# A gated convolution and attention block: the input projection as Strassen products of halves, attention as a stage of its own, the convolution's sum in PSUM

## Chip, cores and metric

One core of one Trainium2 chip. The kernel is one program that reads its inputs from HBM and writes one output there. The metric is the device time of one execution in microseconds; lower is better. Engines are named as in the profile: PE multiplies matrices (PEld loads its weights), DVE and POOL work on vectors, ACT applies functions and copies, SP issues most DMAs. SBUF is the working memory, PSUM holds what PE writes.

## What is computed

`x` has 1024 positions of 1024 channels, all float32. One layer, cut to what matters:

```python
h = rms_norm(x, g_pre)
glu_in, gate_a, q, k, v, gate_b, merge = split(h @ w_in)      # 9216 columns
a, b = split(glu_in)
u = depthwise_causal_conv(a * sigmoid(b), conv_w, 31 taps) + conv_b
y_a = (silu(layer_norm(u, ln_g, ln_b)) * silu(gate_a)) @ w_conv_proj
# 8 heads, two softmax maps each, keys of the same or earlier chunks of 64;
# the first 16 of 64 dims of q and k are rotated by the position
p1, p2 = softmax(q1 @ k1.T / 8), softmax(q2 @ k2.T / 8)
o = rms_norm((p1 - lam * p2) @ v, g_subln) * (1 - lambda_init)
y_b = (o * silu(gate_b)) @ w_attn_proj
m_a, m_b = split(merge)
out = (sigmoid(m_a) * y_a + sigmoid(m_b) * y_b) @ w_out
return x + rms_norm(out, g_post)
```

## The kernel before

**Precision.** PE reads float32 in a rounded form (`fp32r`). Each factor is therefore split into an upper part (H) and what is left (L), and each product is three: H with H, H with L, L with H (`product`, lines 235 to 241). A split is a copy on ACT and a subtraction, on POOL for weights (lines 213, 214).

**Projection.** The normalised `x` is transposed and split once: eight tiles `hH` and eight `hL`, each 128 channels by 1024 positions (lines 287 to 291). The 9216 columns of `w_in` come in blocks of 128 (`weight_blocks`). A block takes, for each half of the positions, 8 contraction tiles x 3 products of 128 x 512 (`project`). The values are the exception: they are wanted with the positions on the partitions, so `hH` and `hL` are the stationary side there, and the products are 256 columns wide (`values`). After each block DVE and ACT turn the sum in PSUM into a gate, a gated unit or rotated queries and keys. Queries and keys go to DRAM whole and are split after they are read back, by ACT and POOL (`stacks`, lines 400 to 403).

**Convolution.** `conv` (lines 607 to 617) adds 31 shifted, scaled copies of a tile of 128 channels, one DVE instruction over 1024 positions for each tap. Input, running sum and output lie in SBUF. It is called at a low priority, so that it fills DVE's gaps.

**Heads.** `head` takes two blocks of 128 queries at a time. For each block and map: scores in PSUM, their maximum (line 441), the exponential with its sum (444); then the second map is scaled by ACT (450), the two are joined by DVE (451), transposed by PE (458), split by ACT and DVE (460, 461) and multiplied by the values (470). The squares for the norm are split (478, 480) and summed over channels by PE with a matrix of ones (481, 482); the norm's factor is applied after all heads (649).

**Order.** `PLAN` names groups of projection blocks; one group follows each pair of heads, so that projection and attention run beside each other. Layer norm, the convolution's gate and attention's projection (`attn_out`) come after the last heads, then the convolution's projection and the output projection. The instructions of each engine stand in a fixed order that a planner writes from estimated times and from priorities. All loads and nearly all stores are issued from SP's queue, in order too. Weights are made one block ahead.

Of the kernel before, what the change touches and what calls it, by code (L numbers as in the profile page):

```python
# [11 lines left out]
F32 = mybir.dt.float32  # L12
# [8 lines left out]
P = 128  # L21
# [19 lines left out]
def weight_blocks():  # L41
    """Order of the projection's column blocks: name -> (index, columns, contraction tiles)."""
    blocks = []
    for p in range(4):
        maps = [(2 * p + i // 2, i % 2) for i in range(4)]
        q0 = [OFF_Q + h * P + m * HD for h, m in maps]
        k0 = [OFF_K + h * P + m * HD for h, m in maps]
        rope = [b + half * 8 + j for half in range(2) for j in range(8) for b in q0 + k0]
        rest = [b + d for d in range(ROPE, HD) for b in q0 + k0]
        blocks.append((("qk", p, 0), rope, range(8)))  # L50
        for n in range(3):
            blocks.append((("qk", p, n + 1), rest[n * P:(n + 1) * P], range(8)))
        cols = list(range(OFF_V + p * 256, OFF_V + (p + 1) * 256))
        blocks.append((("v", p, 0), cols, range(0, 4)))
        blocks.append((("v", p, 1), cols, range(4, 8)))
    for name, off in (("a", OFF_A), ("b", OFF_B), ("ga", OFF_GA), ("gb", OFF_GB),
                      ("ma", OFF_MA), ("mb", OFF_MB)):
        for i in range(8):
            blocks.append(((name, i), list(range(off + i * P, off + (i + 1) * P)), range(8)))
    return blocks  # L60


@with_exitstack
def block_kernel(ctx, tc, x, positions, vecs, conv_w, lambdas, g_subln, g_post,
                 w_in, w_cp, w_ap, w_out, out):
    nc = tc.nc
    sb = lambda name, bufs=1: ctx.enter_context(tc.tile_pool(name=name, bufs=bufs))
    const = sb("const")
    hpool = sb("hpool", 16)
    wpool = sb("wpool", 2)  # L70
    half = sb("half", 6)
    tmp_pool = sb("tiny", 4)
    upool = sb("upool", 2)
    cpool = sb("cpool", 1)
    dram = ctx.enter_context(tc.tile_pool(name="dram", bufs=1, space=DRAM))
    ps = ctx.enter_context(tc.tile_pool(name="ps", bufs=2, space=PSUM))
# [4 lines left out]
    PLAN = ("v0 g0 g1|"  # L81
# [5 lines left out]

    def psum_g():
        return ps.tile([P, HALF], F32, name="ps_g", tag="g", bufs=2)

    def psum_s():
        return ps.tile([P, 2, HALF], F32, name="ps_s", tag="s", bufs=2)

    def halftile(name="hf", tag="hf", bufs=4):
        return half.tile([P, HALF], F32, name=name, tag=tag, bufs=bufs)

    def sidetile(name, dt=F32):
        return half.tile([P, 256], dt, name=name, tag="ha", bufs=6)

# [12 lines left out]
    lamv = apool.tile([P, 4, HD], F32, name="lamv", tag="K", bufs=2)  # L112
# [9 lines left out]
    ones_er = const.tile([P, P], F32R, name="ones_er")  # L122
# [4 lines left out]
    pat = half.tile([P, 2, 8, 8], F32, name="pat", tag="hf", bufs=4)  # L127
# [7 lines left out]
    pat2 = half.tile([P, 16, 8], F32, name="pat2", tag="hf", bufs=4)  # L135
# [6 lines left out]
    nc.vector.memset(col[64:128, 2:3], -1.0)  # L142

# [1 line left out]
    lam = const.tile([P, 4], F32, name="lam")  # L145
    ltmp = half.tile([P, 2, HD], F32, name="ltmp", tag="hf", bufs=4)
# [10 lines left out]
    def rsqrt_small(v, r):  # L157
        """r = v ** -0.5 for a few columns: root of the reciprocal, then one Newton step."""
# [11 lines left out]
    wsrc = {}  # L170
    for i, (key, _, _) in enumerate(weight_blocks()):
        wsrc[key] = w_in[i]
    for i in range(8):
        wsrc[("ap", i)] = w_ap[i]
        wsrc[("cp", i)] = w_cp[i]

    def group(name, *idx):
        return [(name, i) for i in idx]

    def pair(p):  # L180
        return [("qk", p, n) for n in range(4)]

    def vpair(p):
        return [("v", p, 0), ("v", p, 1)]

    def glus(*idx):
        return [(n, i) for i in idx for n in ("b", "a")]

    def parse(text):
        keys = []  # L190
        for tok in text.split():
            k, i = tok[0], int(tok[1])
            keys += {"u": glus(i), "q": pair(i), "v": vpair(i), "g": group("gb", i), "m": group("ma", i),
                     "n": group("mb", i), "s": group("ga", i), "p": group("ap", i)}.get(k, [(k, i)])
        return keys

    plan = [parse(x) for x in PLAN.split("|")]
    start = [("qk", 0, n) for n in (1, 2, 3, 0)] + plan[0]
    head_fill = plan[1:]
    order = start + sum(head_fill, [])  # L200
    order = [k for k in order if k[0] not in "tlw"] + group("cp", *range(8))
    loaded = {}
    nextw = [0]
    AHEAD = 2

    def split(src, wH, wL, eng=None, parts=1):
# [3 lines left out]
        n = D // parts  # L210
        for c in range(parts):
            sl = slice(c * n, (c + 1) * n)
            nc.scalar.copy(out=wH[:, sl], in_=raw[:, sl])  # L213
            (eng or nc.gpsimd).tensor_tensor(out=wL[:, sl], in0=raw[:, sl], in1=wH.bitcast(F32)[:, sl],  # L214
                                             op=ALU.subtract)

    def load_weight(parts=1):
        if nextw[0] >= len(order):
            return
        key = order[nextw[0]]  # L220
        nextw[0] += 1
        wL = wpool.tile(blk, F32R, name="wL", tag="wL")
        wH = wpool.tile(blk, F32R, name="wH", tag="wH")
        split(wsrc[key], wH, wL, parts=2 if key[0] == 'v' and key[2] == 1 else parts)
        loaded[key] = (wH, wL)

    def weight(key):
# [3 lines left out]
        while nextw[0] < len(order) and len(loaded) < AHEAD - 1:  # L231
            load_weight()
        return r

    def product(acc, lH, lL, rH, rL, n=8, tiles=None):
        """acc += sum over (some of) the n contraction tiles of l.T @ r, both in two parts."""
        for d in tiles or range(n):
# [572 lines left out]
```

## Time and profile before

| | us |
|---|---|
| Median of 3 runs | 1339.72 |
| Lowest and highest run | 1338.58, 1340.38 |
| Span of the profiled execution, first to last instruction | 1333.2 |

The profile gives for the profiled execution its span alone; 6.5 us lie between that and the median of the runs. A group of the profile names line, engine and operation, the tile written and the tiles read, shapes, then count, busy time and mean duration in ns, and the engine's idle time before it. Matmuls overlap in the pipeline, so the distance of their starts, not their duration, is what one costs. By stages: the first 32 us bring `x` in and normalise it, from there to 985 us projection and heads run together, then the attention output is normalised and the convolution's branch follows, the convolution's projection among it, and the output projection ends the kernel.

### The profile page before, as it was taken

What the parts mean: (1) busy time and instruction counts of PE and PEld (TensorE: products, weight loads), DVE (VectorE), ACT (ScalarE), POOL (GpSimd) and SP (SyncE); (2) the same over time, 40 slices, a digit from 0 to 9 for tenths busy, and PEclk for the clock granted to TensorE, in tenths of its full rate; (3) what the DMA queues carried; (4) which work ended last, traced back from release to release, by engine and by line L of the source; (5) the groups of instructions that cost most, each with busy time, mean ns of one, the idle gap of its engine ahead of it and who ended that gap; (6) DMA issues with size and microseconds to landing.
All of it is one profiled execution on the core that took longest, in us unless ns stands there. A gap on an engine that the chain in (4) does not pass through costs nothing.

```text
span 1333.2 us, 16733 instructions
## 1 busy us (share of the span) xinstructions
PE 1258.1 (94%) x6352; PEld 1060.5 (80%) x6352; DVE 938.6 (70%) x1267; ACT 509.5 (38%) x926; POOL 375.1 (28%) x170
## 2 busy tenths in 40 slices
PE   4999998989998999999899999999999889999998
PEld 3898876868886887987778888888888668887886
DVE  6513699999969979998996695658616881256433
ACT  5424533532254354224435413656534431122211
POOL 2142232243215115212521422241122453233000
PEclk9999999989998999999899999999999999999999
DMA  5342223342123324122324515144349774345222
GB/s 197 122 145 81 88 83 111 107 138 81 58 87 111 115 91 134 64 64 73 118 76 139 154 60 174 64 135 154 127 156 327 235 258 173 115 154 175 91 84 95
DMA packets 61944, 167.16 MB, mean 125 GB/s; under 512 B 7924, under 2 KB 12580, under 8 KB 61864
## 3 DMA queue, kind: packets, MB, share of 16 engines
q1 hardware_dynamic: 61544, 165.82, 38.2%
q8 instruction: 50, 0.82, 0.3%
q10 hardware_dynamic: 288, 0.26, 0.1%
q14 instruction: 30, 0.25, 0.1%
q0 software_dynamic: 32, 0.02, 0.0%
HBM read 123.00 MB, written 43.07 MB: 125 GB/s over the span
## 4 chain that ended last, share of the span: by engine, by line
PE 44%; DVE 38%; DMA 6%; issue 5%; ACT 2%; POOL 1%; SPq 0%; DVEq 0%; ACTq 0%; POOLq 0%
DVE cv L615 23%; PE ps_g L239 10%; PE ps_g L241 10%; PE ps_g L240 10%; DVE nm L441 2%; PE ps_s L724 2%; PE ps_s L725 2%; PE ps_s L726 2%; PE ps_av L470 2%; DVE wtL L461 2%; PE ps_s L435 1%; PE ps_s L436 1%; DVE e L451 1%; DMA qkraw<-qk_dram 1%; PE ps_t L458 1%
## 5 line engine op out<-in xcount | busy, mean ns | idle before, releaser
L214 POOL TENSOR_TENSOR wL<-wraw,wH 128x1024 fp32r<-128x1024 f32 (+1 forms) x93 | 237.9, 2560 | 674.7 <-ACT wH L213 655.5
L239 PE MATMUL ps_g<-hH,wH 128*128 128x512 f32 (+1 forms) x1040 | 408.4, 393 | 13.2 <-DVE qkst L363 4.7
L241 PE MATMUL ps_g<-hH,wL 128*128 128x512 f32 (+1 forms) x1040 | 406.5, 391 | 0.0
L240 PE MATMUL ps_g<-hL,wH 128*128 128x512 f32 (+1 forms) x1040 | 406.3, 391 | 0.0
L615 DVE SCALAR_TENSOR_TENSOR cv<-u,cw,cv 128x1024 f32<-128x1024 f32 x240 | 375.5, 1565 | 2.6
L239 PEld LDWEIGHTS ps_g<-hH,wH 128*128 128x128 f32 x1040 | 196.9, 190 | 54.6 <-DVE qkst L363 5.6
L241 PEld LDWEIGHTS ps_g<-hH,wL 128*128 128x128 f32 x1040 | 197.1, 190 | 38.3
L240 PEld LDWEIGHTS ps_g<-hL,wH 128*128 128x128 f32 x1040 | 197.1, 190 | 37.7 <-issue 0.5
L444 ACT ACTIVATE e<-ps_s,nm 128x256 f32<-128x256 f32 (+7 forms) x128 | 94.9, 742 | 136.2 <-DVE nm L441 108.3
L213 ACT CAST wH<-wraw 128x1024 fp32r<-128x1024 f32 (+1 forms) x93 | 92.7, 1001 | 125.4 <-PE ps_g L240 89.4
L450 ACT ACTIVATE e<-e,rz 128x128 f32<-128x128 f32 (+3 forms) x64 | 49.7, 777 | 122.2 <-DVE rz L449 121.8
L441 DVE TENSOR_REDUCE nm<-ps_s 128x1 f32<-128x640 f32 (+7 forms) x128 | 94.6, 747 | 1.6
L451 DVE SCALAR_TENSOR_TENSOR e<-e,rz 128x128 f32<-128x128 f32 (+3 forms) x64 | 60.4, 943 | 27.2 <-ACT e L450 27.1
L435 PE MATMUL ps_s<-kst,qh 128*128 128x384 f32 (+4 forms) x192 | 66.7, 353 | 4.2 <-ACT e L444 4.2
L461 DVE TENSOR_TENSOR wtL<-ps_t,wtH 128x512 fp32r<-128x512 f32 (+2 forms) x96 | 52.5, 547 | 19.9 <-ACT wtH L460 19.8
L436 PE MATMUL ps_s<-kst,ql 128*128 128x384 f32 (+4 forms) x192 | 64.6, 342 | 0.0
L460 ACT CAST wtH<-ps_t 128x512 fp32r<-128x512 f32 (+2 forms) x96 | 45.6, 475 | 47.4 <-PE ps_t L458 47.1
L492 ACT ACTIVATE th<-ps_g 128x512 f32<-128x512 f32 x80 | 47.3, 593 | 30.4 <-PE ps_g L241 30.2
L239 PE MATMUL ps_g<-ogH,wH 128*128 128x512 f32 x128 | 50.5, 394 | 6.5 <-DVE yb L591 5.9
L458 PE MATMUL ps_t<-ident,e 128*128 128x128 f32 x288 | 49.8, 277 | 6.5 <-DVE wtL L461 4.6
L401 POOL TENSOR_TENSOR kst<-qkraw,kst 64x1024 fp32r<-64x1024 f32 x16 | 44.4, 2774 | 30.7 <-ACT kst L400 20.7
L239 PE MATMUL ps_g<-zH,wH 128*128 128x512 f32 x128 | 49.9, 390 | 1.3 <-DVE tar L707 1.3
(197 smaller groups left out, 2058.4 us busy)
## 6 DMA issues: line engine op xcount, KB each, us to landing
wraw<-w_in SPq DMA_DIRECT2D x72, 512.0 KB, 3.6
qkraw<-qk_dram SPq DMA_DIRECT2D x64, 256.0 KB, 4.2
qk_dram<-qkst SPq DMA_DIRECT2D x32, 256.0 KB, 2.4
xt<-x SPq DMA_DIRECT2D x8, 512.0 KB, 8.2
o_dram<-og SPq DMA_DIRECT2D x32, 128.0 KB, 1.8
u_dram<-th SPq DMA_DIRECT2D x16, 256.0 KB, 2.0
u<-u_dram SPq DMA_DIRECT2D x8, 512.0 KB, 3.8
cv_dram<-cv SPq DMA_DIRECT2D x8, 512.0 KB, 2.6
```

The lines of the kernel that those rows point to most:

```text
L213: nc.scalar.copy(out=wH[:, sl], in_=raw[:, sl])
L214: (eng or nc.gpsimd).tensor_tensor(out=wL[:, sl], in0=raw[:, sl], in1=wH.bitcast(F32)[:, sl], op=ALU.subtract)
L239: nc.tensor.matmul(acc, a, c, start=(d == 0), stop=False)
L240: nc.tensor.matmul(acc, a, e, start=False, stop=False)
L241: nc.tensor.matmul(acc, b, c, start=False, stop=(d == n - 1))
L435: nc.tensor.matmul(sv[:, a, :], qh[:, qs], k[:, ks], start=True, stop=False)
L436: nc.tensor.matmul(sv[:, a, :], ql[:, qs], k[:, ks], start=False, stop=True)
L441: nc.vector.tensor_reduce(out=nm[:, m:m + 1], in_=sv, op=ALU.max, axis=AX.XY, negate=True)
L444: nc.scalar.activation(out=e[:, :n].rearrange("p (a b) -> p a b", a=c), in_=sv, func=AF.Exp, bias=nm[:, m:m + 1], accum_out=Z[:, m:m + 1])
L451: nc.vector.scalar_tensor_tensor(out=es[0][:, :n], in0=es[0][:, :n], scalar=rz[:, 0:1], in1=es[1][:, :n], op0=ALU.mult, op1=ALU.add)
L461: nc.vector.tensor_tensor(out=wtL[g][:, :nk, us], in0=pt[:, :nk, :], in1=wtH[g].bitcast(F32)[:, :nk, us], op=ALU.subtract)
L615: nc.vector.scalar_tensor_tensor(out=a, in0=u[:, k:k + T], scalar=cw[:, i, k:k + 1], in1=a, op0=ALU.mult, op1=ALU.add)
```

## The change

**Seven products of halves.** Two blocks of 128 columns form a pair. Its weights are a matrix of 2 x 2 quarters A (two blocks by two halves of the contraction), the transposed `x` one of 2 x 2 quarters B (halves of the contraction by halves of the positions). The variant used has seven products in place of eight:

- on the side of `x`, made once: T1 = B12 - B11, T2 = B22 - T1, T3 = B22 - B12, T4 = T2 - B21; these and B11, B21, B22 are split
- on the side of the weights, for each pair, by POOL: S1 = A21 + A22, S2 = S1 - A11, S3 = A11 - A21, S4 = A12 - S2; these and A11, A12, A22 are split (ACT and POOL)
- the seven products are combined by ACT and DVE to the four quarters of the result

```diff
+    def factors(tok):
+        raws = []
+        for key in pair_of(tok):
+            raw = proj.tile(blk, F32, name="wraw", tag="raw", bufs=3)
+            nc.sync.dma_start(out=raw, in_=wsrc[key])
...
+        def made(src):
+            f = proj.tile([P, 2, HALF], F32R, name="wf", tag="wf", bufs=8)
+            split(src, f)
...
+        yield made(a11)
+        s1 = total(a21, a22, ALU.add)
+        s2 = total(s1, a11, ALU.subtract)
+        yield made(s2)
+        yield made(total(a11, a21, ALU.subtract, out=a21))
+        yield made(s1)
+        yield made(a12)
+        yield made(a22)
+        yield made(total(a12, s2, ALU.subtract))
...
+    USED = ("B11", "T2", "T3", "T1", "B21", "T4", "B22")
+    def quarters(tok, left, refill):
...
+        step(p1, 0, True)
+        nc.scalar.activation(out=u2, in_=p1, func=AF.Copy, scale=pos)
+        step(p6, 1, True)
+        plus(u2, p6, u2)
+        step(p7, 2, True)
+        plus(u3, p7, u2)
+        step(p5, 3, True)
+        plus(c22, p5, u3)
+        use(i, 1, 1, c22)
+        step(p1, 4, False)
+        step(p4, 5, True)
+        plus(u3, p4, u3, neg)
+        use(i, 1, 0, u3)
+        use(i, 0, 0, p1)
+        step(p5, 6, False)
+        plus(u2, p5, u2)
+        use(i, 0, 1, u2)
+        if k == "u":
+            with tc.high_priority(offset=-20000):
+                conv(i)
```

`made` splits (a copy on ACT, a subtraction on POOL). `step` issues one product, 4 tiles x 3 matmuls of 512 columns, and then has one factor of the next pair made. `plus` is one DVE instruction with one input in PSUM.

The values go through the same products and are then transposed by PE in blocks of 128 (64 transposes in all). Queries, keys and values are split in this stage, and both parts go to DRAM. The products have six banks of PSUM.

**Convolution.** The running sum is a PSUM tile; each tap reads one input from SBUF and one from PSUM. The layer norm's sums and differences move from DVE to POOL, its passes stand between the later pairs:

```diff
-    PLAN = ("v0 g0 g1|"
...
+PLAN = ("u0 g0 u1 g1 q0 u2 q1 q2 u3 q3 q4 u4 q5 q6 u5 q7 s0 u6 s1 s2 u7 s3 v0 v1 v2 v3 "
+        "l0 m0 l1 m1 l2 m2 m3 n0 n1 g2 g3 n2 n3")
...
+        acc = ps.tile(blk, F32, name="cacc", tag="cv", bufs=1)
+        a = wide("cv", "cv", 1)
...
+        for k in range(1, TAPS):
+            nc.vector.scalar_tensor_tensor(out=a if k == TAPS - 1 else acc, in0=u[:, k:k + T],
+                                           scalar=cw[:, i, k:k + 1], in1=acc, op0=ALU.mult, op1=ALU.add)
```

Here u is the gated unit, q queries and keys, s and g the gates, v the values, m and n the merge gates, l the three passes of the layer norm and the convolution's swish.

**Second stage.** After the last pair all pools of that stage are given back, and the eight heads follow. Beside them stands only the convolution's projection (`conv_out`), one or two blocks after each of the heads 0 to 5. The head reads K, Q, V and its gate ready made, joins the two maps without normalising them first, and norms its own output:

```diff
-                nc.scalar.activation(out=es[1][:, :n], in_=es[1][:, :n], func=AF.Copy, scale=rz[:, 1:2])
-                nc.vector.scalar_tensor_tensor(out=es[0][:, :n], in0=es[0][:, :n], scalar=rz[:, 0:1],
-                                               in1=es[1][:, :n], op0=ALU.mult, op1=ALU.add)
+                nc.vector.reciprocal(out=rz[:, 0:1], in_=Z[:, i, 1:2])
+                nc.vector.scalar_tensor_tensor(out=rz[:, 1:2], in0=rz[:, 0:1], scalar=Z[:, i, 0:1], in1=neglam,
+                                               op0=ALU.mult, op1=ALU.mult)
+                nc.vector.scalar_tensor_tensor(out=es[0][:, :n], in0=es[1][:, :n], scalar=rz[:, 1:2],
+                                               in1=es[0][:, :n], op0=ALU.mult, op1=ALU.add)
...
+            nc.gpsimd.tensor_copy(out=sh, in_=sq)
+            nc.gpsimd.tensor_tensor(out=sl_, in0=sq, in1=sh.bitcast(F32), op=ALU.subtract)
+            for u in range(2):
+                us_ = slice(u * P, (u + 1) * P)
+                nc.tensor.matmul(av[:, 1, 2 * u:2 * u + 2], sh[:, us_], ones_er, start=True, stop=False)
+                nc.tensor.matmul(av[:, 1, 2 * u:2 * u + 2], sl_[:, us_], ones_er, start=False, stop=True)
...
+        nc.sync.dma_start(out=ors_dram[h:h + 1, :].rearrange("o (a p) -> p (o a)", p=P), in_=r)
+        rb = apool.tile(blk, F32, name="orb", tag="rb", bufs=1)
+        nc.sync.dma_start(out=rb, in_=ors_dram[h:h + 1, :].broadcast_to([P, T]))
+        nc.gpsimd.tensor_tensor(out=og, in0=og, in1=rb, op=ALU.mult)
```

**Third stage.** Attention's projection (for the first two blocks all heads but the last come first), merged with the convolution's, then the output projection as before.

More of the change, by code (lines that the diff above doesn't have):

```diff
@@ L167, in rsqrt_small @@
         nc.vector.tensor_tensor(out=r, in0=y, in1=q, op=ALU.mult)
[L170 to L200, printed above, removed]
@@ new lines, in block_kernel, with run, refill @@
+    store = {0: ready + list(early)}
+    def run(n):
+        nxt = factors(pairs[n + 1]) if n + 1 < len(pairs) else iter(())
+        store[n + 1] = []
+        def refill():
+            store[n + 1].extend(f for f in [next(nxt, None)] if f is not None)
+        quarters(pairs[n], store.pop(n), refill)
+    done = 0
+    for tok in plan:
+        if tok[0] == "l":
+            ln_part(int(tok[1]))
+        else:
+            if tok == "q0":
+                tables()
+            run(done)
+            done += 1
@@ new lines, in block_kernel, with psum_2, psum_s @@
+    work_cm.__exit__(None, None, None)
+    proj_cm.__exit__(None, None, None)
+    ps_cm.__exit__(None, None, None)
+    wpool = sb("wpool", 2)
+    half = sb("half", 4)
+    bpool = sb("bpool", 16)
+    apool_cm = tc.tile_pool(name="attn", bufs=1)
+    apool = apool_cm.__enter__()
+    ps_cm = tc.tile_pool(name="ps2", bufs=1, space=PSUM)
+    ps = ps_cm.__enter__()
+    def psum_2():
+        return ps.tile(hb, F32, name="ps_g", tag="g", bufs=2)
+    def psum_s():
+        return ps.tile([P, 2, HALF], F32, name="ps_s", tag="s", bufs=2)
@@ L206, in split, with split2 @@
-    def split(src, wH, wL, eng=None, parts=1):
+    def split2(src, wH, wL, eng=None):
         raw = wpool.tile(blk, F32, name="wraw", tag="wr", bufs=2)
         nc.sync.dma_start(out=raw, in_=src)
[L210 to L225, printed above, removed]
+        nc.scalar.copy(out=wH, in_=raw)
+        (eng or nc.gpsimd).tensor_tensor(out=wL, in0=raw, in1=wH.bitcast(F32), op=ALU.subtract)
@@ L230, in weight @@
         r = loaded.pop(key)
-        while nextw[0] < len(order) and len(loaded) < AHEAD - 1:
+        if not loaded:
             load_weight()
         return r
-    def product(acc, lH, lL, rH, rL, n=8, tiles=None):
-        for d in tiles or range(n):
-            a, b, c, e = lH(d), lL(d), rH(d), rL(d)
-            nc.tensor.matmul(acc, a, c, start=(d == 0), stop=False)
-            nc.tensor.matmul(acc, a, e, start=False, stop=False)
-            nc.tensor.matmul(acc, b, c, start=False, stop=(d == n - 1))
@@ new lines, in block_kernel, with psum_3 @@
+    fill = {0: (0,), 1: (1, 2), 2: (3,), 3: (4, 5), 4: (6,), 5: (7,)}
+    for h in range(8):
+        if h == 6:
+            for g in range(6):
+                load_og(g)
+        head(h)
+        for i in fill.get(h, ()):
+            conv_out(i)
+    ps_cm.__exit__(None, None, None)
+    apool_cm.__exit__(None, None, None)
+    cpool = sb("cpool")
+    ypool = sb("ypool", 16)
+    opool = sb("opool", 8)
+    ps = ctx.enter_context(tc.tile_pool(name="ps3", bufs=8, space=PSUM))
+    def psum_3():
+        return ps.tile(hb, F32, name="ps_o", tag="o", bufs=8)
@@ L726, in out_part @@
             nc.tensor.matmul(acc, yL[d][:, ts], woH[d][:, nsl], start=False, stop=(d == 7))
-    halves = [slice(0, HALF), slice(HALF, D)]
-    both = [psum_s() for _ in range(2)]
+    both = [[psum_3() for _ in range(2)] for _ in range(2)]
     for d0, d1 in ((0, 4), (4, 8)):
@@ L739, in block_kernel @@
         if t < 2:
-            accs = [both[t][:, n, :] for n in range(2)]
+            accs = both[t]
         elif t < NT - 1:
-            acc = psum_s()
-            accs = [acc[:, n, :] for n in range(2)]
+            accs = [psum_3() for _ in range(2)]
             for n in range(2):
```

805 lines of the change are left out of this document (412 added, 393 removed), and 5 rows, old and new, of the table PLAN.

## The prediction

> **What bounds the kernel now.** I read the page first: busy shares, the slices, the chain of work that ended last.
>
> ```profile
> span 1333.2 us, 16733 instructions
> PE 1258.1 (94%) x6352; PEld 1060.5 (80%) x6352; DVE 938.6 (70%) x1267; ACT 509.5 (38%) x926; POOL 375.1 (28%) x170
> ...
> PE 44%; DVE 38%; DMA 6%; issue 5%; ACT 2%; POOL 1%; SPq 0%; DVEq 0%; ACTq 0%; POOLq 0%
> ```
>
> TensorE (PE) is busy for 1258.1 us, so 75 us of the span are its idle time. Yet VectorE (DVE) holds 38% of the chain. The windows of 50 us say where that is (columns: PE, weight loads, DVE, ACT, POOL, each with its count, then the clock).
>
> ```profile
> 0.00:50.00 50.00, 31.31 (x199) 28.15 (x200) 32.89 (x76) 26.96 (x47) 9.01 (x23) 1.00 0.42 156
> ...
> 250.00:300.00 50.00, 43.23 (x196) 35.08 (x195) 49.76 (x44) 20.70 (x33) 21.29 (x7) 0.93 0.45 129
> ...
> 400.00:450.00 50.00, 44.53 (x210) 36.31 (x209) 49.67 (x51) 19.49 (x33) 22.15 (x9) 0.93 0.36 108
> ...
> 1100.00:1150.00 50.00, 50.00 (x220) 40.99 (x220) 6.18 (x9) 5.91 (x6) 14.20 (x7) 1.00 0.41 147
> ...
> 1300.00:1350.00 50.00, 26.56 (x139) 22.36 (x137) 11.69 (x34) 5.00 (x17) 0.00 (x0) 0.96 0.19 63
> ```
>
> Three things are to be seen. PE loses 18.7 us in the first 50, and 33.2 - 26.6 = 6.6 us at the end. Between them it is full, except where DVE is full too (49.76 and 49.67 of 50): there PE loses 5 to 7 us a window. And 1100 to 1150 is pure 512-wide matmuls: 50 / 220 = 0.227 us each. So PE's work sets the time, and DVE's convolution costs some PE on top.
>
> **PE's work.** Groups by shape, and two neighbours in the timeline:
>
> ```profile
> L239 PE MATMUL ps_g<-hH,wH 128*128 128x512 f32 x1008 | 399.4, 396 | 13.1 <-DVE qkst L363 4.7 <-DVE sg L517 2.8 <-ACT th L492 2.4
> ...
> L239 PE MATMUL ps_g<-wH,hH 128*128 128x256 f32 x128 | 37.0, 289 | 0.3 <-DVE vL L385 0.3
> ```
> ```profile
> 28.84 0.29 PE L239 MATMUL ps_g<-hH,wH 128*128 128x256 f32 x1
> 28.96 0.28 PE L240 MATMUL ps_g<-hL,wH 128*128 128x256 f32 x1
> ```
>
> The durations (396, 289 ns) overlap; the starts count: 0.227 us for 512 columns, 0.12 for 256. The projection is now 3 x 1008 = 3024 wide ones (687 us) and 768 (the values) + 96 narrow ones (104 us). After: 36 pairs x 7 products x 12 = 3024 wide ones, 687 us. (Today's work is 3024 + 864 / 2 = 3456 wide ones; 7/8 of that is 3024.) The loops leave no doubt about the count; PE is spared the 104 us of the narrow ones. Added: 64 transposes of the values, between 0.12 us (as a narrow one) and 0.23: 8 to 15, I take 8. The other three projections (1152 wide ones) keep 262 us. What is left of the 1258 is 1258 - 791 - 262 = 205: some 190 for the heads.
>
> **What pays for it: POOL.** A pair needs 4 sums and 7 splits, 11 half-row operations on POOL; a block of before needed one full one.
>
> ```profile
> L214 POOL TENSOR_TENSOR wL<-wraw,wH 128x1024 fp32r<-128x1024 f32 x83 | 222.4, 2680 | 632.6 <-ACT wH L213 613.4 <-PE ps_s L436 19.0
> ```
> ```profile
> 72.24 1.29 POOL L364 TENSOR_TENSOR qkst<-qkst,ropet 128x512 f32<-128x512 f32 x1 [4.30 <-DVE qkst L363]
> ...
> 254.10 3.53 POOL L214 TENSOR_TENSOR wL<-wraw,wH 128x1024 fp32r<-128x1024 f32 x1 [12.38 <-ACT wH L213]
> ...
> 1138.97 2.40 POOL L214 TENSOR_TENSOR wL<-wraw,wH 128x1024 fp32r<-128x1024 f32 x1 [8.59 <-ACT wH L213]
> ```
>
> Undisturbed a full one takes 2.40 us, a half one 1.29; at 254 one took 3.53. DVE's line at that time:
>
> ```profile
> 255.51 3.21 DVE L615 SCALAR_TENSOR_TENSOR cv<-u,cw,cv 128x1024 f32<-128x1024 f32 x1
> ```
> ```profile
> L615 DVE SCALAR_TENSOR_TENSOR cv<-u,cw,cv x240: 1196/1284/3496, 163.5 to 799.1; 128x1024 f32<-128x1024 f32 x120
> ```
>
> A tap takes 1.28 us in the median and 3.2 beside POOL: the two hold each other up. Both inputs of that tap lie in SBUF. Beside a DVE operation with one input in PSUM neither is held up:
>
> ```profile
> 866.35 0.69 DVE L527 SCALAR_TENSOR_TENSOR th<-th,ps_g 128x512 f32<-128x512 f32 x1 [0.95 <-ACT th L492]
> ```
> ```profile
> 866.31 2.41 POOL L403 TENSOR_TENSOR ql<-qkraw,qh 128x1024 fp32r<-128x1024 f32 x1
> ```
>
> The taps' running sum moves to PSUM, so they become of that kind, and I take POOL at its undisturbed price. POOL's work in the first stage: 36 x 11 + 32 (queries and keys) = 428 half operations and 31 full ones (sums, mean and variance of the layer norm) = 486 halves. At 1.29 us that is 627 us, 91% of PE's 695. Raw weights have three buffers; a pair's second block waits for the last sum of the pair before it, so POOL idles some 1.5 us a pair (3.6 us of landing less two half operations, by the row below): 54 us more. So POOL comes close to PE, and the layer norm's mean pass puts 36 us of it into four pairs. With one pair of factors made ahead I put PE's loss at 15 us (0 to 60).
>
> By the Trainium skill (GPSIMD Engine Reference, Key points), GpSimd shares its SBUF interfaces with VectorE and contends with instructions there that have two SBUF inputs. The rows at 254 agree; by this rule the taps in PSUM would not contend at all, and the sum would stay as it is.
>
> **What pays for it: DVE.**
>
> ```profile
> L441 DVE TENSOR_REDUCE nm<-ps_s 128x1 f32<-128x1024 f32 x16 | 19.4, 1215 | 0.1
> ...
> L441 DVE TENSOR_REDUCE nm<-ps_s 128x1 f32<-128x512 f32 x16 | 10.9, 680 | 0.2
> ...
> L503 DVE SCALAR_TENSOR_TENSOR th<-th,ps_g 128x512 f32<-128x512 f32 x16 | 10.8, 678 | 1.6 <-PE ps_g L241 1.4
> ```
>
> A tap with its sum in PSUM is not in the trace. From a 512-wide operation on PSUM and SBUF (0.678) and the reductions' step (1.215 - 0.680), it is 1.21 us; twice 0.678 gives 1.36 at most; I take 1.25. Then 248 taps take 310 us. Before the layer norm (26 pairs, 497 us of PE) DVE has also 26 x 5 combinations (88 us), and about 75 us in gates, rotary, values and tables: 473, 95% of PE's time. DVE's queue is in a fixed order, and in the two full windows above such a load cost PE 5 to 7 us in 50. I put PE's loss at 20 us (0 to 45). PSUM's six banks for products hide a late combination of up to about two products; beyond that PE stops.
>
> **Start.**
>
> ```profile
> 21.69 0.80 PE L239 MATMUL ps_g<-hH,wH 128*128 128x256 f32 x2
> ...
> 39.23 1.43 DVE L289 SCALAR_TENSOR_TENSOR hL<-ps_s,vec,hH 128x512 fp32r<-128x512 f32 x2 [1.74 <-ACT hH L288]
> 40.70 1.43 DVE L289 SCALAR_TENSOR_TENSOR hL<-ps_x,vec,hH 128x512 fp32r<-128x512 f32 x2
> ```
> ```profile
> wraw<-w_in SPq DMA_DIRECT2D x72, 512.0 KB, 3.6
> ...
> or<-ors_dram SPq DMA_DIRECT2D x8, 512.0 KB, 5.5
> ```
>
> Now the projection begins at 21.7 us with the first half of the positions. After, only the first product can; the second needs T2, made from both halves, so it waits for the last of x, which before was split by 42.1 us (last row). For the second half DVE then has 18 operations of about 0.7 us (four splits, eight first differences, T2's four sums, two of its splits) where it had 8: 7 us more, of which waits like the 1.74 us in the first row take up some 3. So the second product starts at 46 us (42 to 55); until then PE has only transposes and one product (3 us).
>
> **Heads.** They are a stage of their own, with only the convolution's projection (384 matmuls, 87 us) beside them: PE has 190 + 87 = 277 us. DVE's rows of the heads:
>
> ```profile
> L441 DVE TENSOR_REDUCE nm<-ps_s 128x1 f32<-128x640 f32 (+7 forms) x128 | 94.6, 747 | 1.6
> L451 DVE SCALAR_TENSOR_TENSOR e<-e,rz 128x128 f32<-128x128 f32 (+3 forms) x64 | 60.4, 943 | 27.2 <-ACT e L450 27.1
> ...
> L461 DVE TENSOR_TENSOR wtL<-ps_t,wtH 128x512 fp32r<-128x512 f32 (+2 forms) x96 | 52.5, 547 | 19.9 <-ACT wtH L460 19.8
> ```
> ```profile
> L449 DVE TENSOR_TENSOR rz<-rz,lam 128x1 f32<-128x1 f32 x64 | 28.0, 437 | 1.2
> ...
> L480 DVE TENSOR_TENSOR osql<-osq,osqh 128x256 fp32r<-128x256 f32 x32 | 22.0, 689 | 0.0
> L440 DVE MEMSET ps_s<- 64x64 f32 x128 | 14.0, 112 | 26.9 <-PE ps_s L436 20.3 <-ACT e L444 5.7
> ...
> L475 DVE TENSOR_TENSOR og<-ps_av,sg 128x256 f32<-128x256 f32 x32 | 13.3, 417 | 18.9 <-ACT osq L473 18.9
> ...
> L448 DVE RECIPROCAL rz<-Z 128x2 f32<-128x2 f32 x64 | 10.1, 158 | 14.7 <-ACT e L444 14.4
> ```
>
> They sum to 295 us. L480 goes to POOL (-22); small norm operations come (+16, at L448's price) and the convolution's 16 merges and last splits (+14): 303 us, or about 275 were none held up. So here DVE is the longest. ACT's scaling of the second map (L450) goes, which only shortens the chain. No filler is left for DVE, where today the taps fill every gap; the two score buffers let two query blocks run together. At a head's end the next one's second map waits for free K and Q buffers (1.5 MB). I take 303 us at 92%: 330 (290 to 420).
>
> ```profile
> GB/s 197 122 145 81 88 83 111 107 138 81 58 87 111 115 91 134 64 64 73 118 76 139 154 60 174 64 135 154 127 156 327 235 258 173 115 154 175 91 84 95
> ```
>
> K, Q and V now come already split: 12 loads of 256 KB, V and the gate, 4.5 MB a head, and with z, weights and stores some 65 MB in the stage, 197 GB/s. A slice of today reaches 327 GB/s, so I cost them at nothing; at a head's start, where nothing covers them, they are the bubble that the 92% holds. In the first stage the stores of Q, K and V double (96 of 256 KB); they share SP's queue with weight loads that now wait for a raw buffer, and whatever stands behind such a load waits too, so that the six small work buffers come free late. That costs nothing while POOL keeps its pair of factors ahead; otherwise it is part of the 60 us above. Change of pools before the heads: the first K and Q land in some 4 us after their space is free: 5 us (0 to 20).
>
> **Rest.** Attention's and the output projection: 768 x 0.227 = 175 us, of which I let 12 run in the last head's gaps. The last head's norm chain (a write, the 5.5 us broadcast, POOL, ACT, DVE: some 14 us) lies beside 84 products (19 us). End: 6.6.
>
> **Sum.** 46 + (687 - 3 + 8) + 35 + 5 + 330 + 163 + 7 = 1278 us of span. The median of the runs, 1339.7, stands 6.5 over the span of 1333.2, so **1285**.
>
> **Rivals.**
> 1. Everything hides: stage-one loss 5, no bubble, heads 290, 160 for the rest: 1200 + 6.5 = 1207. For it: PE was at 50.00 of 50 beside a DVE of 30 to 47 us. Against: POOL at 91% and DVE at 95%. 0.20.
> 2. Slower: taps and POOL still hold each other up. Then a half operation costs 2.680 / 2.40 x 1.29 = 1.44 us on average, up to 1.9 (3.53 / 2.40). At 1.56, between, 486 x 1.56 + 54 = 812 us of POOL against 727: 1285 + 85 = 1370. It decides once a half operation passes (695 - 54) / 486 = 1.32 us. 0.13.
> 3. Slower: the heads wait for their own chain (scores, maximum, exponential, sum, transpose), DVE at 72%: 420 us, 1375. For it: no filler. Against: two score buffers. 0.12.
> 4. Slower: PE's clock falls in the heads.
>
> ```profile
> 274.00:278.00 4.00, 1.00 (x5) 0.48 (x3) 3.96 (x2) 1.79 (x3) 3.84 (x3) 0.85 0.53 150
> 278.00:282.00 4.00, 3.12 (x12) 2.93 (x13) 4.00 (x5) 0.00 (x0) 2.70 (x1) 0.50 0.51 135
> 282.00:286.00 4.00, 4.00 (x16) 3.20 (x15) 4.00 (x5) 2.20 (x4) 0.00 (x0) 0.80 0.22 73
> ```
>
> After a gap the granted clock was 0.50, then 0.80: 2.0 + 0.8 = 2.8 us lost. At each of the 32 steps of two query blocks that makes 90 us: 1375, if PE ends last there. Against: DVE does. 0.05. The Trainium skill (TensorE: Matmul & The Clock Gate, the HAM clock gate) says that an idle window of about 3.4 us halves the clock; the rows agree.
>
> The forecast has 0.50, by itself 1245 to 1325. The range over all but the outer tenths is 1210 to 1370. A difference of 0.2% (2.7 us) is about what a measurement can tell. Rivals 2 to 4 hold 0.30; where they strike at under half their price the kernel is still faster (0.05) or equal (0.02). So faster 0.75, same 0.02, slower 0.23.
>
> **What would show it.** Second product near 46 us; PE over 90% to about 770 us, in windows with 0.227 us a matmul; L615's successor near 1.25 us with max and median close; POOL's halves near 1.29; heads near 330 us with DVE over 90%. Wrong would be: halves over 1.4 (rival 2), DVE under 75% in the heads (3), a clock under 0.9 there (4).

## The result: 15% slower, and the profile after

| | before | after |
|---|---|---|
| Median of the runs, us | 1339.15 (1337.09 to 1340.38) | 1544.05 (1542.77 to 1546.25) |
| Span of the profiled execution, us | 1333.2 | 1542.5 |
| Mean granted clock of PE | 0.989 | 0.894 |

The ratio is 1.152, 95% interval 1.149 to 1.155. The forecast was 1285, the range 1210 to 1370. The page of the changed kernel, its busy shares, PE's slices with the clock, and the chain that ended last:

```profile
span 1542.5 us, 16543 instructions
PE 1249.0 (81%) x5616; PEld 1036.0 (67%) x5616; DVE 962.8 (62%) x1490; ACT 549.0 (36%) x1026; POOL 795.8 (52%) x598
...
PE   2799999899999998089989299895665676689998
...
PE 39%; DMA 14%; POOL 14%; DVE 8%; issue 6%; ACT 5%; SPq 1%; POOLq 0%; DVEq 0%; ACTq 0%
```

PE was busy 94% before and is busy 81% now, and DVE has nearly left the chain (38% to 8%), while DMA (6% to 14%) and POOL (1% to 14%) hold more of it. Three places stand out among the slices: the 0 in the middle, the 2 after it, and the stretch of 5 to 7 that follows. The windows of the changed kernel, cut at those places (PE, weight loads, DVE, ACT, POOL, each with its count; clock; DMA share; GB/s):

```profile
0.00:54.00 54.00, 19.94 (x74) 15.51 (x75) 41.55 (x79) 33.97 (x62) 26.83 (x36) 1.00 0.36 132
61.00:611.00 550.00, 527.76 (x2317) 432.82 (x2317) 494.39 (x495) 195.48 (x333) 455.61 (x347) 0.98 0.38 130
611.00:663.00 52.00, 0.71 (x3) 0.41 (x2) 0.69 (x1) 6.73 (x8) 32.33 (x17) 0.53 0.23 76
663.00:849.00 186.00, 178.97 (x760) 145.14 (x759) 70.06 (x75) 69.28 (x112) 138.05 (x91) 0.97 0.45 156
849.00:880.00 31.00, 3.10 (x8) 2.01 (x8) 1.57 (x5) 6.91 (x7) 11.66 (x5) 0.56 1.00 287
880.00:1058.00 178.00, 160.13 (x783) 135.24 (x784) 98.06 (x246) 71.13 (x153) 44.47 (x33) 0.89 0.54 157
1058.00:1345.00 287.00, 173.19 (x856) 151.82 (x857) 168.19 (x441) 122.80 (x273) 53.44 (x55) 0.71 0.41 110
1345.00:1543.00 198.00, 182.46 (x812) 151.40 (x811) 81.29 (x144) 39.50 (x76) 28.90 (x13) 0.96 0.35 117
```

Against the terms of the forecast (heads from their first matmul at 867 to their end near 1350):

| Stretch | forecast, us | measured, us |
|---|---|---|
| start, until the products run steadily | 46 | 61 |
| products of stage 1, losses included | 727 | 788, of which 51 are one stop |
| change of stages | 5 | 18 |
| heads | 330 | 483 |
| rest and end | 170 | 192 |
| span | 1278 | 1542 |

So 153 of the 264 us lie in the heads, 51 in one stop of PE. The heads are of two kinds: on PE all 384 matmuls of the convolution's projection ran between 906 and 1039, beside heads 0 and 1, whose norms leave at 960 and 1047, with PE 90% busy from 880 to 1058; heads 2 to 7 had nothing beside them, and there PE is busy 60% (173.19 of 287 us). Who was waited for stands in the timelines of PE, POOL and SP's queue (start, duration, engine, line, tiles, in brackets the idle time before and its releaser). PE at the stop, at the first matmul of the heads, and at the start of a head in the middle:

```profile
662.59 3.78 PE L421 MATMUL ps_g<-tot,ones_d 128*128 128x512 f32 x4 [51.29 <-POOL tot L439]
...
867.14 0.77 PE L674 MATMUL ps_s<-kst,qh 128*128 128x128 f32 x2 [18.24 <-ACT zH L579]
...
1122.42 0.45 PE L674 MATMUL ps_s<-kst,qh 128*128 128x128 f32 x1 [9.25 <-DMA qh<-qkh]
```

POOL before the stop, and SP's queue before that head:

```profile
647.59 2.34 POOL L434 TENSOR_TENSOR cvr<-cvr,mu 128x1024 f32<-128x1024 f32 x1 [3.38 <-DMA cvr<-cv]
651.09 2.34 POOL L439 TENSOR_TENSOR tot<-tot,cvr 128x1024 f32<-128x1024 f32 x1 [1.17 <-ACT cvr L435]
656.70 2.34 POOL L434 TENSOR_TENSOR cvr<-cvr,mu 128x1024 f32<-128x1024 f32 x1 [3.27 <-DMA cvr<-cv]
```
```profile
1102.46 0.37 SPq L729 DMA_DIRECT2D ors_dram<-orr  x1
1111.41 0.32 SPq L731 DMA_DIRECT2D orb<-ors_dram  x1
1111.82 0.45 SPq L638 DMA_DIRECT2D qh<-qkh  x1
1112.36 0.57 SPq L638 DMA_DIRECT2D kst<-qkh  x1
```

The stop: the matmul that sums the variance stands in PE's queue ahead of the next pair's products, and POOL prepares its input one tile in 9.1 us (647.59 to 656.70: wait for the load, subtract, square on ACT, add; POOL itself works 4.7 us of it). The head: SP writes the norm's factor at 1102.46, the broadcast that reads it back stands in the queue until 1111.41, and the next head's K and Q loads stand behind it.

### The profile page after: what moved, and what is told of

Same layout as the page of the kernel before. It is cut to its first block, busy times and chain, and to the rows that moved or that the text cites. A ratio compares the mean times of both kernels' runs of the same rounds, so it can differ in the third digit from the quotient of the medians.

```text
span 1542.5 us, 16543 instructions
## 1 busy us (share of the span) xinstructions
PE 1249.0 (81%) x5616; PEld 1036.0 (67%) x5616; DVE 962.8 (62%) x1490; ACT 549.0 (36%) x1026; POOL 795.8 (52%) x598
## 4 chain that ended last, share of the span: by engine, by line
PE 39%; DMA 14%; POOL 14%; DVE 8%; issue 6%; ACT 5%; SPq 1%; POOLq 0%; DVEq 0%; ACTq 0%
PE ps_g L471 16%; PE ps_o L604 6%; PE ps_g L604 5%; POOL wf L183 5%; DMA ors_dram<-orr 3%; POOL wsum L202 2%; DMA wraw<-ogd 2%; PE ps_av L710 2%; PE ps_o L822 2%; PE ps_o L823 2%; PE ps_o L821 2%; DVE cacc L408 2%; ACT e L683 2%; POOL qkL L377 2%; DMA ql<-qkl 2%
## 5 line engine op out<-in xcount | busy, mean ns | idle before, releaser
L471 PE MATMUL ps_g<-T,wf 128*128 128x512 f32 x1728 | 406.1, 390 | 4.6 <-DVE T L276 3.9
L471 PEld LDWEIGHTS ps_g<-T,wf 128*128 128x128 f32 x1728 | 324.9, 188 | 73.0 <-DVE T L276 4.3
L471 PE MATMUL ps_g<-B,wf 128*128 128x512 f32 x1296 | 320.5, 400 | 23.8 <-DVE c L483 23.7
L471 PEld LDWEIGHTS ps_g<-B,wf 128*128 128x128 f32 x1296 | 249.4, 193 | 82.0 <-DVE c L483 28.0
L408 DVE SCALAR_TENSOR_TENSOR cacc<-u,cw,cacc 128x1024 f32<-128x1024 f32 x232 | 297.6, 1283 | 2.8
L183 POOL TENSOR_TENSOR wf<-wraw,wf 128x512 fp32r<-128x512 f32 x144 | 198.1, 1379 | 53.8 <-ACT wf L182 53.8
L183 POOL TENSOR_TENSOR wf<-wsum,wf 128x512 fp32r<-128x512 f32 x108 | 149.0, 1380 | 20.3 <-ACT wf L182 20.3
L483 DVE SCALAR_TENSOR_TENSOR u<-ps_g,u 128x512 f32<-128x512 f32 x112 | 76.7, 685 | 80.3 <-PE ps_g L471 75.7
L182 ACT CAST wf<-wraw 128x512 fp32r<-128x512 f32 x144 | 88.5, 618 | 104.6 <-PE ps_g L471 77.7
L717 POOL CAST osqh<-osq 128x256 fp32r<-128x256 f32 x32 | 13.8, 432 | 175.5 <-ACT osq L713 168.8
L680 DVE TENSOR_REDUCE nm<-ps_s 128x1 f32<-128x128 f32 (+7 forms) x128 | 95.2, 750 | 1.7
L732 POOL TENSOR_TENSOR og<-og,orb 128x1024 f32<-128x1024 f32 x8 | 18.8, 2353 | 97.4 <-DMA orb<-ors_dram 68.0
L202 POOL TENSOR_TENSOR wsum<-wraw 128x512 f32<-128x512 f32 x36 | 48.4, 1345 | 37.9 <-DMA wraw<-w_in 37.1
```

Source lines behind the costliest of these rows:

```text
L182: nc.scalar.copy(out=f[:, 0, :], in_=src)
L183: nc.gpsimd.tensor_tensor(out=f[:, 1, :], in0=src, in1=f.bitcast(F32)[:, 0, :], op=ALU.subtract)
L202: nc.gpsimd.tensor_tensor(out=t, in0=in0, in1=in1, op=op)
L408: nc.vector.scalar_tensor_tensor(out=a if k == TAPS - 1 else acc, in0=u[:, k:k + T], scalar=cw[:, i, k:k + 1], in1=acc, op0=ALU.mult, op1= ...
L471: nc.tensor.matmul(acc, f[:, l, sl], b[:, r, :], start=(start and d + n == 0), stop=False, skip_group_check=True)
L483: nc.vector.scalar_tensor_tensor(out=out, in0=acc, scalar=pos if s is None else s, in1=u, op0=ALU.mult, op1=ALU.add)
```

## The experiments

The theories: **A**, the variance holds PE's queue; **B**, the norm's write at each head's end holds SP's queue; **C**, the heads standing alone wait for their own chain (rival 3 of the prediction); **D**, against B: whichever queue holds the norm, the head needs it as long. The letters inside the recorded expectations are their own. Times are medians; ratios are to the kernel before on the same chip.

**1. The variance named three pairs later (A).**

```diff
-        "l0 m0 l1 m1 l2 m2 m3 n0 n1 g2 g3 n2 n3")
+        "l0 m0 m1 m2 m3 l1 n0 l2 n1 g2 g3 n2 n3")
```

> The second pass of the layer norm (variance, l1) is named three pairs later in the plan, and the last pass (l2) after it; nothing else differs. Theory A (PE's fixed queue): the variance's matrix product stood in PE's queue 51 us before its sum was ready, and nothing behind it could pass; later in the plan the wait is gone: about 1544 - 50 = 1494 us, with PE over 90% busy between 600 and 700 us. Rival B (the time comes back): the last pass now ends later, the convolution's projection or the first head waits for z instead: 1535 to 1550 us, with a new wait of 40 to 50 us at the change of stages. Rival C (POOL is the limit there: its queue is full of layer norm work and PE waits for factors anyway): gain under 20 us.

1515.96, ratio 1.132 (1.123 to 1.141): 28 us come back, where A forecast 50. The stop and the first matmul of the heads are now:

```profile
684.99 3.42 PE L421 MATMUL ps_g<-tot,ones_d 128*128 128x512 f32 x4 [17.34 <-POOL tot L439]
839.64 0.77 PE L674 MATMUL ps_s<-kst,qh 128*128 128x128 f32 x2 [23.05 <-DMA qh<-qkh]
```

The stop shrinks from 51.29 us to 17.34, and the heads begin at 839.64 instead of 867.14. So A is the cause of the part that came back, but the wait isn't gone, and some 5 us of the gain go at the next barrier (23.05 us against 18.24).

**2. The norm's write and broadcast from POOL's queue (B against D).**

```diff
-        nc.sync.dma_start(out=ors_dram[h:h + 1, :].rearrange("o (a p) -> p (o a)", p=P), in_=r)
+        nc.gpsimd.dma_start(out=ors_dram[h:h + 1, :].rearrange("o (a p) -> p (o a)", p=P), in_=r)
...
-        nc.sync.dma_start(out=rb, in_=ors_dram[h:h + 1, :].broadcast_to([P, T]))
+        nc.gpsimd.dma_start(out=rb, in_=ors_dram[h:h + 1, :].broadcast_to([P, T]))
```

> The write and the broadcast read of each head's norm factor are issued from POOL's queue in place of SP's; nothing else differs. Theory A (SP's fixed queue): at each head's end SP waits some 11 us for the write of 4-byte pieces to land before it may issue the broadcast, and the next head's K and Q loads stand behind it; off that queue the loads go out at once: seven head ends of about 11 us, 1544 - 75 = 1470 us (1455 to 1500). Rival B (the heads wait for their own chain of scores, maximum, exponential, sum and transpose): under 20 us are gained, the distance from head to head stays near 53 us. Rival D (POOL, now waiting, holds the squares of the next head and through them PE): no gain or slower.

1550.32, ratio 1.158 (1.146 to 1.169): nothing gained, as D forecast. The waits of this run (engine, line, releaser: total us, times, longest):

```profile
POOL orb L731 <- DMA ors_dram<-orr: 67.7, 8, 10.0
...
PE ps_av L721 <- POOL osqh L717: 33.6, 10, 8.0
```

POOL now stands 8.5 us in the mean (10.0 at most) for the write at a head's end, with the next head's squares (L717) behind it and PE behind those. D holds: the wait has moved from SP's queue to POOL's.

Naming the next head's loads ahead of the norm (1545.08, ratio 1.154, where about 1470 was forecast if B held) didn't tell the two apart: the planner issued write, broadcast and loads in the same order (1102.01, 1110.44, 1110.85).

**3. Deeper K and Q buffers.** K 3 to 4, Q 6 to 8, paid for with one buffer of `e` and two of the small tiles.

> K has four buffers in place of three and Q eight in place of six, so that a whole head's K and Q can be loaded while the head before it runs (for the space the exponentials have three buffers in place of four, the squares four in place of six). Theory A/E (what is late at a head's start is the second map's K and Q, for want of a buffer, an early place in SP's queue or bandwidth): the waits for K and Q go, 12 to 18 us at each of seven heads: 1544 - 100 = 1444 us (1420 to 1480). Rival B (the heads' own chain): within 15 us of 1544, the distance from head to head stays near 53 us.

1549.25, ratio 1.157 (1.152 to 1.162): nothing gained, where about 1444 was forecast. The loads are there in time now (from 867 to 1351 PE's waits for K and Q between the first scores and the last fall from 39 us to 8.5), yet the heads' writes leave SP at 1095.33, 1149.68 and 1204.35, 54 to 55 us apart, as before. The largest wait of PE in 1058 to 1345 in their place (17.5 us before):

```profile
PE ps_av L721 <- POOL osqh L717: 49.1, 9, 9.9
```

Behind the write stand two queues: SP's with the loads and POOL's, where the product with the broadcast (L732) precedes the next head's squares. With one of them mended the other ends last. That is an argument from the waits: the run also has one buffer of `e` less, and PE's wait for the exponentials grew too (33.5 to 45.4 us in the same stretch), so C explains part of it as well.

**4. The write itself made short.** PE transposes the factor, 128 x 8, and it is written as 8 rows of 512 B, not as 1024 pieces of 4 B.

```diff
-        nc.sync.dma_start(out=ors_dram[h:h + 1, :].rearrange("o (a p) -> p (o a)", p=P), in_=r)
+        rt = ps.tile([P, 4, P], F32, name="ps_t", tag="t", bufs=1)
+        nc.tensor.transpose(out=rt[0:8, 0, :], in_=r, identity=ident)
+        rr = side("orrow")[0:8, 0:P]
+        nc.scalar.copy(out=rr, in_=rt[0:8, 0, :])
+        nc.sync.dma_start(out=ors_dram[h:h + 1, :].rearrange("o (a p) -> (o a) p", p=P), in_=rr)
```

> Each head's norm factor (128 x 8) is transposed by PE and copied by ACT, and written as 8 rows of 512 bytes in place of 1024 pieces of 4 bytes; queues and order stay. Theory A (SP waits for that write, and the next head's K and Q loads wait behind it): the write lands in some 2 us in place of 11, so eight heads gain about 8 us each: 1544 - 60 = 1484 us (1470 to 1500). Rival B (the heads' own chain): within 15 us of 1544. Rival E (the loads themselves are what is late: 1.5 MB at each head's end at 100 to 260 GB/s take 6 to 15 us whenever they begin): 20 to 40 us gained, and PE's longest waits in the heads are still for the K and Q loads.

1504.13, ratio 1.123 (1.119 to 1.128): 40 us less, where the expectation had 60 by its theory A and 20 to 40 by its rival E, late loads. The write and the broadcast in SP's queue:

```profile
1084.52 0.29 SPq L733 DMA_DIRECT2D ors_dram<-orrow  x1
1085.91 0.32 SPq L735 DMA_DIRECT2D orb<-ors_dram  x1
```

1.4 us between them instead of 9 (over the eight heads 1.2 to 2.1 instead of 9 to 11); the heads are 45 to 47 us apart, before 51 to 55. With run 2, where the same write stood in another queue and nothing was gained, this says that the duration of the write was the cost, not the queue that it stood in. Rival E isn't excluded as a part: in the heads PE still waits 28 us for K and Q, beside 25 for the exponentials and 20 for the buffer of the transposed weights. Four heads in the windows:

```profile
1039.50:1223.50 184.00, 123.67 (x644) 104.80 (x644) 127.86 (x340) 94.18 (x212) 38.71 (x40) 0.82 0.49 138
```

DVE is busy 69% and PE 67%: neither is full, and 46 us a head remain.

**5. The clock.** 384 matmuls of 512 columns whose results nobody uses were added to the heads. They need 384 x 0.227 = 87 us of PE.

```diff
+                idle = psum_2()
+                for _ in range(6):
+                    nc.tensor.matmul(idle, vH[:, 0, :], vH[:, 0:4, :], start=True, stop=True)
```

> Six matmuls of 512 columns whose result nobody reads stand ahead of the transposes of each of the 64 query blocks: 384 matmuls, 87 us of PE work added, to keep PE's clock up. If the clock is what makes the heads long (rival 4 of the prediction): the granted clock in the heads rises from 0.71 to over 0.9 and the heads take less in spite of the added work, 1544 - 30 to - 60 us. If the heads wait for loads and for their chain: the clock rises, the heads take the same or more (added matmuls stand ahead of transposes in PE's queue): 1544 to 1600 us.

1581.15, ratio 1.181 (1.176 to 1.186): 37 us more. In 1058 to 1345 PE's clock rises from 0.71 to 0.85, short of the 0.9 forecast, and the heads don't get shorter:

```profile
1058.00:1345.00 287.00, 224.17 (x1140) 191.70 (x1139) 161.79 (x401) 111.28 (x248) 53.62 (x50) 0.85 0.43 121
```

The low clock follows from the gaps: filling them raised it. The 87 us of added work cost 37, so 50 found room, in the gaps or in what the higher clock saved; the run can't part the two. It shows that the clock can't be bought back this way, not what a full clock without added work would be worth.

**6. Eight plain products in place of seven.** Factors as they are, no sums on POOL, the rest of the change kept.

> Each pair of blocks by eight plain products of halves in place of seven: no sums of weights or of x, four splits a pair in place of seven, no combinations on DVE; all else, the plan and the heads among it, is the same. If the seven products are worth their count: 36 x 12 x 0.227 = 98 us more of PE, less some 10 to 15 us at the start (no T2 to wait for): about 1625 us. If POOL and DVE set the pace of the first stage as much as PE does (the sums and combinations cost what the products save): within 20 us of 1544. If the combinations cost more than they save: below 1525 us.

1576.91, ratio 1.178 (1.170 to 1.186). So the seven products are worth 33 us in the whole, between the forecasts (about 1625, or within 20 us of 1544). Their count, 432 matmuls fewer, is 98. With eight, PE is full in the first stage:

```profile
50.00:500.00 450.00, 450.00 (x1987) 372.60 (x1986) 333.04 (x302) 111.24 (x184) 164.59 (x128) 1.00 0.36 118
```

With seven it loses 22 us of 550 there (528 busy) and starts later (24.12 us of PE in the first 50 with eight, 15.94 with seven). The stop at the variance is in both, 46.17 us here. The stage alone shows more than 33: with eight the heads' first matmul comes at 918.16, 51 us after the 867.14 with seven. The heads of the run with eight, whose code is the same, are then 49 to 50 us apart against 51 to 55, which takes 18 us back for a reason that no run separates.

**7. Attention apart from the projection, in the kernel before.** Only its plan is changed: units, queries, keys and one set of merge gates stand ahead of the first head, so that the heads of three pairs have just the next pair's values and gates beside them.

```diff
-    PLAN = ("v0 g0 g1|"
-            "u2 u0 q1 u1 m0 g3 m1 v1 g2|"
-            "u3 q2 u4 u5 m2 v2 g4 m3 g5|"
-            "u6 q3 m5 u7 m4 m7 m6 v3 g6 g7|"
+    PLAN = ("u2 u0 q1 u1 m0 m1 u3 q2 u4 u5 m2 m3 u6 q3 m5 u7 m4 m7 m6 v0 g0 g1|"
+            "v1 g2 g3|"
+            "v2 g4 g5|"
+            "v3 g6 g7|"
```

> The kernel before, with one thing changed: its plan names the gated units, the query/key blocks and the a-merge gates ahead of the first pair of heads, so that the six heads of the first three pairs have only the next pair's values and gates beside them. Number of matmuls, taps in SBUF, blocks one by one: all as before. Theory (heads that stand alone cost their own chain, some 45 us each, whatever the rest of the change): 6 x 45 = 270 us of heads, less 6 x 24 = 142 of their own PE work and some 44 of gate products that fit in: +85, about 1425, with PE well under 75% and the clock under 0.9 in that stretch. Rival (the cost of the heads after the change lies in its new code, the norm at each head's end and the K and Q loads, and not in standing alone): 1335 to 1360.

1447.51, ratio 1.081 (1.075 to 1.087): 108 us slower with nothing else changed. The same stretch, first of the kernel before, then of this one:

```profile
550.00:650.00 100.00, 96.55 (x498) 81.98 (x497) 90.95 (x121) 37.01 (x74) 28.05 (x13) 1.00 0.25 81
650.00:750.00 100.00, 93.80 (x463) 78.67 (x464) 79.52 (x112) 47.58 (x92) 37.75 (x14) 0.97 0.39 119
```
```profile
550.00:650.00 100.00, 78.11 (x429) 66.54 (x429) 77.33 (x151) 61.59 (x132) 25.11 (x11) 0.86 0.33 98
650.00:750.00 100.00, 84.44 (x479) 71.72 (x477) 61.82 (x143) 57.12 (x129) 19.39 (x9) 0.91 0.18 52
```

PE and DVE both fall, as in the changed kernel, and so does the clock; PE stays at 78 to 84%, above the 75 expected, and the whole costs 23 us more than expected. Over the span PE idles 133 us instead of 75, and 50 of these 58 us lie between 550 and 900, where the heads stand apart; the rest of the loss is that PE is busy 1312 us instead of 1258 for the same 6352 matmuls. This kernel has no write at a head's end and holds its values in SBUF. So C holds by itself, before any new code.

**8. The mends together.** First rows, deeper buffers and the later variance at once; then rows and the later variance without the deeper buffers; then, besides, two PSUM buffers for the transposed weights and one for the convolution's products:

```diff
-        return ps.tile(hb, F32, name="ps_g", tag="g", bufs=2)
+        return ps.tile(hb, F32, name="ps_g", tag="g", bufs=1)
...
-                    pt = ps.tile([P, 4, P], F32, name="ps_t", tag="t", bufs=1)
+                    pt = ps.tile([P, 4, P], F32, name="ps_t", tag="t", bufs=2)
```

> The row-wise write, the deeper K and Q buffers and the later variance together. If the causes are separate, their gains add: 29 us of the later variance (measured), with 60 to 100 of the heads: 1415 to 1455 us, which is still slower than the kernel before. If rival B holds: about 1515 us, no better than the later variance alone.

> The change with two mends at once: the norm's factor written as 8 rows, and the layer norm's mean and variance passes named two blocks later. Each alone gave 40 and 28 us. If they are two waits in two places that do not meet, 1544 - 68 = 1476 (1468 to 1486). If the time saved by the later variance comes back at the change of stages, as part of it did in the run with three mends (1489), 1490 to 1505.

> As the run with the two mends, and in the heads two PSUM buffers for the transposed weights and one for the convolution's products instead of one and two. In the run with rows the PE waited some 25 us in four heads for DVE's second halves to free that buffer, 50 in eight. If that wait is a link of the heads' own chain: 25 to 50 us less than the run with two mends, heads about 40 us apart. If DVE or the exponentials end last in its place: within 8 us of that run, heads still 44 to 46 us apart.

1489.14 (1.112), 1473.98 (1.101, interval 1.093 to 1.108) and 1427.21 (1.066, 1.060 to 1.072). The first missed its forecast: four of its heads take 49.5 us each against 46 with rows alone, so the deeper K and Q gave less than their price, one buffer of `e` and two of the small tiles; which of these it was isn't shown. The second is what the two single gains add up to. The third gains 47 more, inside its forecast of 25 to 50. The one buffer for the transposes was a link of the heads' chain: until DVE has read it for the lower half, PE cannot transpose again, and PE's waits for that fall from 17.3 us (27 times) to 1.5 (4 times). From the third head's end to the seventh's, without and with it:

```profile
1060.21:1243.19 182.98, 124.86 (x644) 106.35 (x644) 129.39 (x340) 95.33 (x213) 40.77 (x41) 0.79 0.48 137
```
```profile
1030.67:1201.63 170.96, 123.80 (x644) 109.06 (x644) 125.69 (x340) 92.71 (x214) 38.75 (x41) 0.76 0.53 148
```

The same 644 matmuls in 171 us instead of 183, at a lower clock. That is 3 us a head, and the heads are 43 us apart where 40 had been forecast. So most of the gain lies elsewhere, and that the total met its forecast is partly luck: 30 us had been won by the end of the third head (1030.67 against 1060.21), where the run's other edit acts too. With one buffer for them the convolution's products reach further into the heads (the last start at 1028 instead of 998) and cover the third head as well. No run parts the two edits.

**9. The change of stages.** z's loads and splits named behind the first head, on top of the last kernel.

```diff
-    for i in range(8):
-        split_z(i)
...
         head(h)
+        if h == 0:
+            for i in range(8):
+                split_z(i)
```

> As the run with two mends and two buffers for the transposed weights (1427), and the loads and splits of z, which are named ahead of the first head, are named behind it. There the first K and Q loads left SP at 829, behind z loads that wait for z's last rows (written at 821), and PE stood still for 23 us. If the order of SP's queue makes that stop: the loads leave some 10 us earlier and the run gives 1407 to 1418. If the loads can't leave earlier in any order, because their space comes free only with the last work of stage 1: 1422 to 1432, the stop unchanged.

1431.28, ratio 1.070 (1.059 to 1.081): no change, as the second forecast had it. The first K load leaves at 829.28 (829.17 without the edit), and PE's first matmul of the heads comes at the same time:

```profile
838.52 0.76 PE L674 MATMUL ps_s<-kst,qh 128*128 128x128 f32 x2 [22.42 <-DMA ql<-qkl]
```

The order of naming isn't what holds it. Until 820 SP stands before a store of the first stage (its tanh comes from ACT then), and z's loads and the convolution's go ahead of K; which of them frees the space for K was not tried apart.

## Why the prediction was wrong

**The step that failed is in Heads: "I take 303 us at 92%: 330".** DVE's work was sized a little high (98 + 168 = 266 us in 880 to 1345, against 303), but it was busy 57% there. PE, taken at 277 us, was busy 341 of the 484 us from 867 to 1351, so no engine was full. The bound was a chain of dependent steps with no cover: the forecast spread the convolution's projection over the heads, and it ran beside the first two. The prediction held this as rival 3 (DVE at 72%, 420 us, 0.12), and its own sign for it, DVE under 75%, came true; 483 us is beyond that rival's price too. It set "two score buffers" against it. That argument failed: in the heads PE waits 40 us for the exponentials, 39 for K and Q, 26 for POOL's squares and 14 for the single transpose buffer, and in the kernel before, with projection work in between, it waits 4.2 us for the exponentials and 4.6 for that buffer. Run 7 prices the separation alone at 108 us.

**The norm's write was costed at the wrong place.** The prediction worked out the chain of a write, a 5.5 us broadcast and a product, "some 14 us", for the last head only. It occurs at all eight, in SP's queue with K and Q behind it and in POOL's with the squares behind it (9 to 11 us each from the write to the broadcast's issue). Made short, it gives 40 us back. That "K, Q and V" can be costed "at nothing" was true of the bandwidth and not of the queue.

**The layer norm was counted as load and not as a wait.** "The layer norm's mean pass puts 36 us of it into four pairs" is right as POOL's work. That PE's queue has a matmul behind that work wasn't said: 51.29 us, of which run 1 won 28.

**Change of stages: 5 (0 to 20), measured 18 to the first matmul**, with 3.10 us of PE work in 849 to 880. **Start: 46, measured 54.7** for the second product's first matmul, steady at 61: a term of the sum that was mis-sized. **Rest and end: 170, measured 192**: the 12 us that were to run in the last head's gaps did not, since attention's projection starts at 1350.73, behind that head, and PE then waits 5.88 us for a weight at 1381.

**The seven products: 104 us of narrow matmuls spared, 35 us of losses, later start.** The count was exact (3024), and the losses were near: apart from the stop PE was busy 707 of the 736 us from 61 to 849, so 29 lost. Against eight products that leaves 51 us of gain at the end of the stage and 33 in the whole (run 6), so even with nothing lost behind, the prize was small beside what the new order put at stake.

**What held.** The taps and POOL, the prediction's main concern, came out as argued:

```profile
L408 DVE SCALAR_TENSOR_TENSOR cacc<-u,cw,cacc 128x1024 f32<-128x1024 f32 x232 | 297.6, 1283 | 2.8
...
L183 POOL TENSOR_TENSOR wf<-wraw,wf 128x512 fp32r<-128x512 f32 x144 | 198.1, 1379 | 53.8 <-ACT wf L182 53.8
...
L182 ACT CAST wf<-wraw 128x512 fp32r<-128x512 f32 x144 | 88.5, 618 | 104.6 <-PE ps_g L471 77.7 <-POOL wraw L202 13.6 <-issue 4.9
```

A tap with its sum in PSUM takes 1.283 us (1.25 taken), against 1.565 for the mean of the taps in SBUF in the kernel before. A half operation of POOL takes 1.38 in the mean, over the 1.32 from which rival 2 was to decide. Yet PE lost only 29 us beside the stop. POOL was busy 83% in 61 to 611 (455.6 of 550 us), so it kept ahead: the copies in front of it waited mostly for PE to give a factor's buffer back (77.7 us), far less for POOL's sums (13.6). Rival 4 came true as a sign (clock 0.71 from 1058 to 1345). As a cause it is not shown: run 5 raised the clock without gain, though with 87 us of work on top, and in run 8 four heads became 12 us shorter while the clock went from 0.79 to 0.76. What the low clock adds to the chain stays open; a transpose takes 340 ns in the mean against 277 before.

**The account.** 1339 - 33 (seven products) + 108 (heads apart) + 40 (the write) + 28 (what a later variance gives back) = 1482 of 1544. The other 62 are, as far as argued, the rest of the variance's stop, the change of stages (28 of 31 us without PE work), the later start and the end; each shows in the windows, none was undone by itself. The terms were measured in different kernels and need not add. Run 7 has six heads with the next pair's values and gates beside them, the changed kernel six with nothing beside them, so its 108 is likely a low value of that term. The best kernel found is 1427 us, 6.6% slower than the kernel before.

## What to carry to other kernels

Before work is taken out from beside a chain of small dependent steps, price that chain without it: here a stage in which DVE was busy 268 us and PE 341 took 483. At every new wait, list what stands behind it in each in-order queue, also PE's and POOL's; a mend in one queue gains nothing while a second one stands behind the same slow transfer. A forecast that rests on an engine at 92% wants a row in which that chain ran by itself, and a reordered plan of the old kernel would have given it.

## What the runs showed of the hardware that was not expected

A store of 4 KB took 10.9 us in the median from issue to landing as 1024 pieces of 4 B (the DMA issues of the changed kernel), while a K or Q block of 256 KB took 6.8:

```profile
qh<-qkh SPq DMA_DIRECT2D x32, 256.0 KB, 6.8
...
ors_dram<-orr SPq DMA_DIRECT2D x8, 4.0 KB, 10.9
```

As 8 rows of 512 B (run 4) the broadcast could follow the same 4 KB after 1.2 to 2.1 us. The Trainium skill (DMA: Bandwidth & Descriptors, Why small descriptors are slow (HBM only)) gives each packet and each descriptor a fixed cost; the two runs agree with it in direction, and that section names no figure for pieces of 4 B.
